# Decay rows moved to ScalarE's DMA queue, with a third raw weight buffer, in a hybrid encoder

## The chip, the core and the metric

The kernel runs on one core of one Trainium2 chip, as one program. The metric is device time in microseconds (us) for one execution, the median of several. Five engines work side by side, each through its own instructions in order: TensorE (PE in the profile; its weight loads are PEld), VectorE (DVE), ScalarE (ACT), GpSimd (POOL) and SyncE (SP), which here only issues DMAs. A DMA may be issued by SP, ACT or POOL, and the instruction that issues it stands in that engine's row like any other.

## The reference, cut to what matters

The program is an encoder of two residual layers over 512 positions of width 1024, in float32. The second ("odd") layer is the one that the change touches. Its input projection gives 24 heads of a bidirectional state-space mixer (SSD) in four groups, and a short gated convolution:

```python
xbc = silu(dw_conv(xbc, conv_w) + conv_b)        # width 5, channels of x, B and C
dA = dt * a;  a_cs = cumsum(dA) in chunks of 128
L = exp(where(tri, a_cs[..., :, None] - a_cs[..., None, :], -inf))
M = (C @ B^T) * L                                # per head and direction
y = M @ X + (states that enter the chunk) ...    # forward + backward + d_skip * x
y = rms_norm(y * silu(z));  out = x + concat(y, short_conv) @ w_out
```

Each entry of L needs the running sum `a_cs` of a head both along rows and along columns. The kernel writes `a_cs` to DRAM once (tile `acs`) and reads each head's two rows (forward and backward, 512 positions each) back into all 128 partitions. That read is the "decay" DMA: `e<-acs`, 512 KB written.

## The kernel before, in words

Weights. Every projection weight is loaded as a slab of 128 x 1024 float32 (`w_raw`, from SP), and split into two parts for TensorE: ACT casts the high part (`w_hi`, line 89). In the odd layer ACT also writes minus the raw slab into `w_lo` (L91) and POOL issues a DMA that adds the raw slab to it (L92). So a raw buffer is free again only when that adding DMA is through. There are two raw buffers (`raw_bufs=2`), three of `w_hi` and of `w_lo`, and every fourth slab of these kinds takes one more pair from the odd layer's pool (`self.more`).

Odd layer. 45 channel tiles go one after the other through `fill`: a projection of 24 matmuls into PSUM (`mm_cm`, L323), and then, for the kinds x, B and C, `conv5`: ACT opens it (L724), DVE adds four taps (L726), ACT takes a tanh (L727), DVE ends it (L728). After the matmuls of the next tile, PE transposes the result (L271 into `sb`). Between the tiles stands the SSD: for each of 24 heads `ssd_factors` makes a 512-wide factor `f`. The decays in `e` get two passes in each of four chunks (ACT L925, DVE L926) and an exponential (ACT L928), `f` starts from `cbm` and `dt` (ACT L920, DVE L921), and DVE multiplies the two (L929). `ssd_pair` then uses the factors of two heads on PE (L942, L958).

Order. A list scheduler sets the order of each engine's instructions when the program is built, from the program's dependencies and its own costs; each engine then runs its list strictly in that order. A wait in front of one instruction holds all that stand behind it on the engine.

Buffers. The decays lie in four `wide` tiles. Before head hh is made, `decays(hh + 2)` issues the loads up to that head from SP's queue. Convolved tiles, their temporaries (`c5`, `c5t`), `sc_h` and some tiles of the end share five buffers of tag `c5`; the factors have four.

Of the kernel before, what the change touches and what calls it, by code (L numbers as in the profile page):

```python
# [6 lines left out]
F32 = mybir.dt.float32  # L7
F32R = mybir.dt.float32r
# [7 lines left out]
P = 128  # L16
S = 512
NT = 4
D = 1024
# [10 lines left out]
SH = 24  # L30
# [36 lines left out]
BY_DMA = ("C", "B", "x", "zc", "h", "gc", "gb", "zd")  # L67
# [3 lines left out]
class Weights:  # L71
# [7 lines left out]
    def _prepare(self):  # L79
        nc = self.tc.nc  # L80
        key, ap, kt, n = self.slabs[self.i]
        eng = nc.vector if key in EARLY or key in ("oe", "oo") and self.i % 2 else nc.gpsimd
        self.i += 1
        raw = self.pool.tile([P, D], F32, name="w_raw", tag="w_raw", bufs=self.raw_bufs)[:, :kt * n]
        nc.sync.dma_start(raw, ap)
        more = key in BY_DMA and self.i % 4 == 0
        hi, lo = ((self.more if more else self.pool).tile([P, D], F32R, name=nm, tag=nm, bufs=1 if more else self.bufs)
                  [:, :kt * n] for nm in ("w_hi", "w_lo"))
        nc.scalar.copy(hi, raw)  # L89
        if key in BY_DMA:  # L90
            nc.scalar.mul(lo, raw, -1.0)  # L91
            nc.gpsimd.dma_start(lo, raw, accum_op=ALU.add)  # L92
        else:
            eng.tensor_tensor(lo, raw, hi.bitcast(F32), op=ALU.subtract)  # L94
        v = lambda t: t.rearrange("p (k n) -> p k n", k=kt)
        self.ready.append((key, v(hi), v(lo)))
# [79 lines left out]
def trunk(ctx, tc, A, out, dbg=None):  # L176
    nc = tc.nc
# [13 lines left out]
    def page(name, tag, dt=F32):  # L191
        return pg.tile([P, S], dt, name=name, tag=tag, bufs=npage[tag])
# [4 lines left out]
    def small(shape, name, bufs=2, dt=F32):  # L197
        return cp.tile(shape, dt, name=name, tag=name, bufs=bufs)
# [26 lines left out]
    def pcs(name, i=None):  # L225
        o, w = PC[name]
        return pc[:, o:o + w] if i is None else pc[:, o + i:o + i + 1]
# [147 lines left out]
    for k in range(KT):  # L375
# [4 lines left out]
        hi, lo = page("xg_hi", "keep", F32R), page("xg_lo", "keep", F32R)  # L380
# [12 lines left out]
    for t in range(NT):  # L393
        for h in range(2):
            j = small([P, S], "junk", bufs=1, dt=BF16)
# [10 lines left out]
    rb = along(r4, "cv")  # L406
# [23 lines left out]
    for nm, o, w in (("q_norm", 0, 384), ("kv_norm", 384, 256)):  # L430
        ss = small([P, 4], "ss")
        rs = small([P, 4], "rs")
        for t in range(NT):
            j = small([P, S], "junk", bufs=1, dt=BF16)
# [6 lines left out]
        for k in range(w // P):  # L441
            tp = transposed([qkv[t][:, o + k * P:o + (k + 1) * P] for t in range(NT)])
            hi, lo = page("cT_hi", "att", F32R), page("cT_lo", "att", F32R)
# [225 lines left out]
    for h in range(2):  # L669
        c = slice(h * S, (h + 1) * S)  # L670
# [37 lines left out]
    def tmp(name, tag, bufs, shape=(P, S), dt=F32):  # L708
        return pg.tile(list(shape), dt, name=name, tag=tag, bufs=bufs)

    def prow(nm):
        return rc[:, RC[nm][0]:RC[nm][0] + RC[nm][1]]
# [6 lines left out]
    def conv5(key, i, c):  # L719

        z = mm_cm(key, xT)
        w = lambda j: pc[:, PC["conv_c_w"][0] + i * 5 + j:PC["conv_c_w"][0] + i * 5 + j + 1]
        d = tmp("c5t", "c5", 5)
        SC.activation(c, z, AF.Identity, scale=w(2), bias=pcs("conv_c_b", i))  # L724
        for j, o, ii in taps5:
            V.scalar_tensor_tensor(c[:, o], z[:, ii], w(j), c[:, o], op0=ALU.mult, op1=ALU.add)  # L726
        SC.activation(d, c, AF.Tanh, scale=0.5)  # L727
        V.scalar_tensor_tensor(c, d, 1.0, c, op0=ALU.add, op1=ALU.mult)  # L728
# [7 lines left out]
    sc = {}  # L736

    def channel_tile(kind, i):
        if kind == "z":
            for t, a in mm_tm("z", xT, 4, GW + NH, four(1)):  # L740
                V.tensor_tensor(dtr[:, t], a[:, GW:GW + NH], prow("dt_bias"), op=ALU.add)
                gate(zg[i][:, t], a[:, :GW])
        elif kind == "zc":
            c = tmp("c5", "c5", 5)
            gate(c, mm_cm("zc", xT))
            turn_later(c, lambda tp: SC.copy(zg[i // 3][:, :, i % 3 * P:(i % 3 + 1) * P], c4(tp)))
        elif kind == "C":
            inp[i]["C"] = tmp("CT", "CT", 2)
            conv5("C", 16 + i, inp[i]["C"])
            inp[i]["x"] = tmp("xs", "xs", 2, (P, NT, GW))  # L750
        elif kind == "B":
            bt = tmp("BT", "BT", 1)
            conv5("B", 12 + i, bt)
            inp[i]["B"] = bt

            def put(tp):
                inp[i]["Bt"] = tmp("Bt", "Bt", 1)
                SC.copy(inp[i]["Bt"], tp)
            turn_later(bt, put)
        elif kind == "x":  # L760
            c = tmp("c5", "c5", 5)
            conv5("x", i, c)
            g, j = divmod(i, 3)
            turn_later(c, lambda tp: SC.copy(inp[g]["x"][:, :, j * P:(j + 1) * P], c4(tp)))
        elif kind == "h":
            sc["h"] = tmp("sc_h", "c5", 5)
            SC.copy(sc["h"], mm_cm("h", xT))
        elif kind == "gc":
            z, hp = mm_cm("gc", xT), sc["h"]
            V.tensor_tensor(hp, z, hp, op=ALU.mult)  # L770
            c = oF[i] = page("oF", "keep")
            SC.activation(c, hp, AF.Copy, scale=cdw[:, i, 1:2])
            for j, o, ii in taps3:
                V.scalar_tensor_tensor(c[:, o], hp[:, ii], cdw[:, i, j:j + 1], c[:, o], op0=ALU.mult, op1=ALU.add)
        elif kind == "gb":
            z = mm_cm("gb", xT)
            V.tensor_tensor(oF[i], z, oF[i], op=ALU.mult)
        else:
            z = mm_cm("zd", xT)
            gate(sc["h"], z)  # L780
            G.tensor_tensor(oF[i], oF[i], sc["h"], op=ALU.mult)
# [18 lines left out]
    d1, d2, d3, dt = (one([P, NT, NH], n) for n in ("d1", "d2", "d3", "dt"))  # L800
# [18 lines left out]
    back = bank("tp")  # L819
    for d in range(2):  # L820
        tp = transposed([d1[:, t, d * SH:(d + 1) * SH] for t in range(NT)], "tp", SH)
        cs = tmp("cs", "c5", 5)[:SH]
        for c in range(NT):
            o, i, z = cs[:, c * P:(c + 1) * P], tp[:, c * P:(c + 1) * P], ident[:SH]
            if d:
                o, i = o[:, ::-1], i[:, ::-1]
            V.tensor_tensor_scan(o, i, z, 0.0, op0=ALU.add, op1=ALU.bypass)
        nc.sync.dma_start(acs[d], cs)
        for c in range(NT):
            T.transpose(back[:, c * NH + d * SH:c * NH + (d + 1) * SH], cs[:, c * P:(c + 1) * P], ident[:SH, :SH])  # L830
# [69 lines left out]
    def decays(n):  # L900

        while len(ahead) <= min(n, SH - 1):
            e = wide("e").rearrange("p (d s) -> p d s", d=2)
            src = acs[:, len(ahead)].rearrange("d (o s) -> o d s", o=1)
            nc.sync.dma_start(e, src.broadcast_to([P, 2, S]))
            ahead.append(e)

    def ssd_factors(g, j, cbm):

        fs = []  # L910
        for i in range(2):
            hh = g * HPG + 2 * j + i
            hf, hb = hh, SH + hh

            decays(hh + 2)
            rb = ahead[hh]
            e, f = rb[:, 0], tmp("f", "f", 4)
            for c in range(NT):
                cc = slice(c * P, (c + 1) * P)
                SC.activation(f[:, cc], cbm[0][:, cc], AF.Copy, scale=dt[:, c, hf:hf + 1])  # L920
                V.scalar_tensor_tensor(f[:, cc], cbm[1][:, cc], dt[:, c, hb:hb + 1], f[:, cc],  # L921
                                       op0=ALU.mult, op1=ALU.add)
            for c in range(NT):
                cc = slice(c * P, (c + 1) * P)
                SC.activation(e[:, cc], rb[:, 0, cc], AF.Identity, bias=nacs[:, c, hf:hf + 1])  # L925
                V.scalar_tensor_tensor(e[:, cc], rb[:, 1, cc], nacs[:, c, hb:hb + 1], e[:, cc],  # L926
                                       op0=ALU.add, op1=ALU.min)
            SC.activation(e, e, AF.Exp)  # L928
            V.tensor_tensor(f, e, f, op=ALU.mult)  # L929
            fs.append(f)  # L930
        return fs

# [50 lines left out]
    def ssd_turn(g):  # L983

        xs = inp[g]["x"]
        for j in range(3):
            i = 3 * g + j
            tp = transposed([xs[:, c, j * P:(j + 1) * P] for c in range(NT)])
            if g < GRP - 1:
                oF[4 + i] = zg[g].rearrange("p c d -> p (c d)")[:, j * S:(j + 1) * S]  # L990
                SC.activation(oF[4 + i], tp, AF.Copy, scale=pcs("ssd_norm", i))
            else:
                hi, lo = tmp("o_hi", *(("c5", 5), ("c5", 5), ("CT", 2))[j], dt=F32R), \
                    tmp("o_lo", *(("c5", 5), ("BT", 1), ("CT", 2))[j], dt=F32R)
                split_psum(hi, lo, tp, pcs("ssd_norm", i))
                last.append((hi, lo))

# [58 lines left out]
    for h in range(2):  # L1056
        c = slice(h * S, (h + 1) * S)
# [98 lines left out]
```

## Time and profile before

| | us |
|---|---|
| median of 3 runs (lowest, highest) | 992.61 (992.29, 994.43) |
| the profiled execution | 995.21 |
| its span in the profile | 993.4 |
| PE, DVE, ACT, POOL busy in the span | 935.8, 694.3, 505.8, 308.4 |

The span is the time from the first to the last instruction in the trace, 1.8 us less than the profiled execution's own time. Matmuls are pipelined in the profile, so a PE that shows as busy need not run at its peak; the granted clock (PEclk, 1.00 is full speed) says how fast it may run. Rows of a timeline give start and duration in us, engine, line, operation, output and inputs, how many instructions were merged, and in brackets how long the engine stood idle just before and what ended that.

### The profile page before, as it was taken

What the parts mean: (1) busy time and instruction counts of PE and PEld (TensorE: products, weight loads), DVE (VectorE), ACT (ScalarE), POOL (GpSimd) and SP (SyncE); (2) the same over time, 40 slices, a digit from 0 to 9 for tenths busy, and PEclk for the clock granted to TensorE, in tenths of its full rate; (3) what the DMA queues carried; (4) which work ended last, traced back from release to release, by engine and by line L of the source; (5) the groups of instructions that cost most, each with busy time, mean ns of one, the idle gap of its engine ahead of it and who ended that gap; (6) DMA issues with size and microseconds to landing.
All of it is one profiled execution on the core that took longest, in us unless ns stands there. A gap on an engine that the chain in (4) does not pass through costs nothing.

```text
span 993.4 us, 12611 instructions
## 1 busy us (share of the span) xinstructions
PE 935.8 (94%) x4528; PEld 754.4 (76%) x4528; DVE 694.3 (70%) x1292; ACT 505.8 (51%) x964; POOL 308.4 (31%) x269
## 2 busy tenths in 40 slices
PE   7899999999999999999997988898999799999996
PEld 7887686686786787888884767777787687888885
DVE  4699989899898998952446678477857658437315
ACT  7646444444454553632334677557657655534312
POOL 0251734626428063551221121121112212125112
PEclk9999999999999999999996989899899989999998
DMA  8213422212203135233367767657756756661222
GB/s 305 102 30 111 57 60 66 62 33 93 70 25 110 62 49 173 64 128 106 118 167 192 174 166 171 148 136 193 180 149 163 189 136 137 170 181 65 105 85 84
DMA packets 48373, 119.57 MB, mean 120 GB/s; under 512 B 12808, under 2 KB 14472, under 8 KB 48312
## 3 DMA queue, kind: packets, MB, share of 16 engines
q1 hardware_dynamic: 41832, 95.19, 30.9%
q0 software_dynamic: 6480, 23.60, 12.7%
q8 instruction: 35, 0.57, 0.2%
q14 instruction: 26, 0.21, 0.1%
HBM read 90.85 MB, written 4.33 MB: 96 GB/s over the span
## 4 chain that ended last, share of the span: by engine, by line
PE 66%; DVE 12%; DMA 11%; ACT 6%; issue 3%; POOL 0%; SPq 0%; DVEq 0%; ACTq 0%; POOLq 0%
PE acc L323 29%; PE acc L350 9%; PE tp L350 5%; PE sb L350 5%; PE sb L534 5%; DMA e<-acs 4%; PE tp L271 4%; DMA w_raw<-in_w_cm_o 3%; PE cv L350 3%; PE acc L571 3%; PE tp L958 2%; ACT w_hi L89 2%; DMA w_lo<-w_raw 1%; DMA w_raw<-in_w_cm_e 1%; PE cv L942 1%
## 5 line engine op out<-in xcount | busy, mean ns | idle before, releaser
L323 PE MATMUL acc<-xT_hi,w_hi 128*128 128x512 f32 x616 | 253.3, 412 | 2.7 <-ACT xT_hi L411 2.7
L323 PE MATMUL acc<-xT_lo,w_hi 128*128 128x512 f32 x616 | 250.0, 407 | 0.2 <-POOL xT_lo L412 0.2
L89 ACT CAST w_hi<-w_raw 128x1024 fp32r<-128x1024 f32 (+7 forms) x139 | 134.6, 969 | 219.7 <-PE acc L323 58.9
L323 PE MATMUL acc<-xT_hi,w_lo 128*128 128x512 f32 x616 | 157.2, 394 | 0.0
L94 DVE TENSOR_TENSOR w_lo<-w_raw,w_hi 128x1024 fp32r<-128x1024 f32 (+6 forms) x74 | 83.2, 1124 | 92.0 <-ACT w_hi L89 83.2
L323 PEld LDWEIGHTS acc<-xT_hi,w_hi 128*128 128x128 f32 x616 | 119.6, 194 | 28.0 <-ACT xT_hi L411 2.9
L323 PEld LDWEIGHTS acc<-xT_lo,w_hi 128*128 128x128 f32 x616 | 119.4, 194 | 25.1 <-POOL xT_lo L412 0.8
L486 DVE SCALAR_TENSOR_TENSOR cv<-u,pc,cv 128x497 f32<-128x497 f32 (+10 forms) x176 | 130.2, 740 | 10.1 <-ACT cv L475 7.7
L323 PEld LDWEIGHTS acc<-xT_hi,w_lo 128*128 128x128 f32 x616 | 116.5, 190 | 24.2
L92 POOL DMA_DIRECT2D w_lo<-w_raw x45 | 39.3, 873 | 226.4 <-ACT w_lo L91 138.5
L94 POOL TENSOR_TENSOR w_lo<-w_raw,w_hi 128x1024 fp32r<-128x1024 f32 (+1 forms) x20 | 48.1, 2406 | 111.7 <-ACT w_hi L89 111.7
L484 POOL TENSOR_TENSOR side<-side 128x510 f32<-128x510 f32 (+3 forms) x56 | 77.8, 1389 | 4.7
L489 POOL TENSOR_TENSOR u<-cs,side 128x512 f32<-128x512 f32 x8 | 11.0, 1372 | 156.3 <-issue 149.1
L538 ACT ACTIVATE p<-sb,mx 128x512 f32<-128x512 f32 x64 | 43.4, 683 | 20.7 <-DVE mx L536 20.4
L483 POOL TENSOR_SCALAR side<-u,pc 128x510 f32<-128x510 f32 (+3 forms) x56 | 51.1, 913 | 4.7
L91 ACT ACTIVATE w_lo<-w_raw 128x1024 fp32r<-128x1024 f32 x45 | 47.6, 1057 | 0.6 <-PE acc L323 0.6
L926 DVE SCALAR_TENSOR_TENSOR e<-e,nacs 128x128 f32<-128x128 f32 x96 | 33.4, 386 | 18.1 <-ACT e L925 18.1
L536 DVE TENSOR_REDUCE mx<-sb 128x1 f32<-128x512 f32 x64 | 41.7, 684 | 3.1 <-PE sb L534 2.5
L726 DVE SCALAR_TENSOR_TENSOR c<-acc,pc,c 128x510 f32<-128x510 f32 (+1 forms) x48 | 35.8, 746 | 11.3 <-ACT c L724 10.7
L925 ACT ACTIVATE e<-e,nacs 128x128 f32<-128x128 f32 x96 | 32.3, 393 | 21.9 <-DMA e<-acs 21.9
L271 PEld LDWEIGHTS tp<-kc,p 128*128 128x128 f32 x256 | 28.9, 140 | 15.4 <-ACT pt L561 10.7
L534 PE MATMUL sb<-k_t,qk_hi 128*128 128x512 f32 (+1 forms) x128 | 39.4, 403 | 0.4 <-DVE k_t L262 0.4
(325 smaller groups left out, 1850.4 us busy)
## 6 DMA issues: line engine op xcount, KB each, us to landing
w_raw<-in_w_cm_o SPq DMA_DIRECT2D x45, 512.0 KB, 3.5
w_lo<-w_raw POOLq DMA_DIRECT2D x45, 512.0 KB, 5.3
w_raw<-in_w_cm_e SPq DMA_DIRECT2D x32, 512.0 KB, 3.5
e<-acs SPq DMA_DIRECT2D x24, 512.0 KB, 5.9
w_raw<-in_w_out_e SPq DMA_DIRECT2D x16, 512.0 KB, 3.5
w_raw<-in_w_out_o SPq DMA_DIRECT2D x16, 512.0 KB, 3.3
xt<-in_xT SPq DMA_DIRECT2D x8, 256.0 KB, 4.2
x_t<-in_x SPq DMA_DIRECT2D x4, 512.0 KB, 5.8
```

Source lines behind the costliest of these rows:

```text
L89: nc.scalar.copy(hi, raw)
L91: nc.scalar.mul(lo, raw, -1.0)
L94: eng.tensor_tensor(lo, raw, hi.bitcast(F32), op=ALU.subtract)
L271: T.transpose(tp[:rows, j * P:(j + 1) * P], b, ident)
L323: T.matmul(a, l, r, start=n == 0, stop=n == 3 * kk - 1)
L350: T.matmul(accs[t][:, :n], l, r, start=k1 == 0 and c == 0, stop=end and c == len(seq) - 1)
L483: G.tensor_scalar(t[:, o], ut[:, i], wt(j), 0.0, op0=ALU.mult, op1=ALU.add)
L484: G.tensor_tensor(side[:, o], side[:, o], t[:, o], op=ALU.add)
L486: V.scalar_tensor_tensor(c[:, o], ut[:, i], wt(j), c[:, o], op0=ALU.mult, op1=ALU.add)
L534: T.matmul(s, l[:, qs], r, start=n == 0, stop=n == 2)
L536: V.tensor_reduce(mx, s, axis=AX.X, op=ALU.max, negate=True)
L538: SC.activation(p, s, AF.Exp, bias=mx, accum_out=sums[:, q:q + 1])
```

## The change

Four things change, all of them in the odd layer:

- the decay rows are loaded by DMAs that ACT issues instead of SP;
- they are loaded three heads ahead: `decays(2)` before the first head, and `decays(hh + 3)` after head hh's multiplication, in place of `decays(hh + 2)` before head hh;
- every third slab of the kinds that the adding DMA serves takes a third raw buffer, from the odd layer's pool;
- `c5` has four buffers instead of five, and `f` three instead of four.

```diff
-        raw = self.pool.tile([P, D], F32, name="w_raw", tag="w_raw", bufs=self.raw_bufs)[:, :kt * n]
+        more = key in BY_DMA and self.i % 3 == 0
+        raw = (self.more if more else self.pool).tile([P, D], F32, name="w_raw", tag="w_raw",
+                                                      bufs=1 if more else self.raw_bufs)[:, :kt * n]
...
-        d = tmp("c5t", "c5", 5)
+        d = tmp("c5t", "c5", 4)
...
-            nc.sync.dma_start(e, src.broadcast_to([P, 2, S]))
+            nc.scalar.dma_start(e, src.broadcast_to([P, 2, S]))
...
-            decays(hh + 2)
+            decays(2)
             rb = ahead[hh]
-            e, f = rb[:, 0], tmp("f", "f", 4)
+            e, f = rb[:, 0], tmp("f", "f", 3)
...
             V.tensor_tensor(f, e, f, op=ALU.mult)
+            decays(hh + 3)
             fs.append(f)
```

The five other places that name `("c5", 5)` change to 4 in the same way. Lines after 84 are two further down in the new file (L905 becomes L907, L925 becomes L927), and those behind the new `decays` call three.

The scheduler makes new lists. Three places show what moves.

The first is SP's list, from the last even-layer stores (`x1d`) to the middle of the odd layer; `acs<-cs` are the two stores that the decay loads read. Before:

```order
L85 DMA w_raw<-in_w_cm_o 128x1024 x5
L828 DMA acs<-cs 24x512
L85 DMA w_raw<-in_w_cm_o 128x1024
L828 DMA acs<-cs 24x512
L85 DMA w_raw<-in_w_cm_o 128x1024
L905 DMA e<-acs 128x2x512 x4
L85 DMA w_raw<-in_w_cm_o 128x1024 x4
L905 DMA e<-acs 128x2x512 x3
```

After:

```order
L87 DMA w_raw<-in_w_cm_o 128x1024 x6
L830 DMA acs<-cs 24x512 x2
L87 DMA w_raw<-in_w_cm_o 128x1024 x34
```

The decay loads are gone from SP, and 34 raw slabs now follow one another there.

The second is ACT's list where the fourth group's C and B tiles are convolved (`CT` and `BT`). Before:

```order
L89 CAST w_hi<-w_raw 128x1024
L724 ACTIVATE CT<-acc,pc 128x512
L91 ACTIVATE w_lo<-w_raw 128x1024
L925 ACTIVATE e<-e,nacs 128x128 x4
L89 CAST w_hi<-w_raw 128x1024
L727 ACTIVATE c5t<-CT 128x512
L928 ACTIVATE e<-e 128x512
L724 ACTIVATE BT<-acc,pc 128x512
```

After:

```order
L907 DMA e<-acs 128x2x512
L726 ACTIVATE CT<-acc,pc 128x512
L93 ACTIVATE w_lo<-w_raw 128x1024
L907 DMA e<-acs 128x2x512
L91 CAST w_hi<-w_raw 128x1024
L729 ACTIVATE c5t<-CT 128x512
L927 ACTIVATE e<-e,nacs 128x128
L726 ACTIVATE BT<-acc,pc 128x512
```

ACT now issues two decay loads here itself, and the first use of the first of them stands five instructions behind its issue, ahead of BT's opening; before, four uses stood ahead of that opening.

The third is ACT's list in the third group, between the openings of two x tiles (`c_6191` and `c_6239` before, `c_6193` and `c_6241` after are the same tiles). Before:

```order
L724 ACTIVATE c_6191<-acc,pc 128x512
L758 COPY Bt<-sb 128x512
L91 ACTIVATE w_lo<-w_raw 128x1024
L89 CAST w_hi<-w_raw 128x1024
L727 ACTIVATE c5t<-c_6191 128x512
L925 ACTIVATE e<-e,nacs 128x128 x2
L724 ACTIVATE c_6239<-acc,pc 128x512
```

After:

```order
L726 ACTIVATE c_6193<-acc,pc 128x512
L93 ACTIVATE w_lo<-w_raw 128x1024
L760 COPY Bt<-sb 128x512
L907 DMA e<-acs 128x2x512
L91 CAST w_hi<-w_raw 128x1024
L729 ACTIVATE c5t<-c_6193 128x512
L927 ACTIVATE e<-e,nacs 128x128
L726 ACTIVATE c_6241<-acc,pc 128x512
```

The decay load is issued between the two openings, and its first use (of the same tile `e`) stands two instructions behind the issue. The fourth group has the same pattern once more, between its second and third x tiles.

More of the change, by code (lines that the diff above doesn't have):

```diff
@@ L743, in channel_tile @@
         elif kind == "zc":
-            c = tmp("c5", "c5", 5)
+            c = tmp("c5", "c5", 4)
             gate(c, mm_cm("zc", xT))
@@ L760, in channel_tile @@
         elif kind == "x":
-            c = tmp("c5", "c5", 5)
+            c = tmp("c5", "c5", 4)
             conv5("x", i, c)
@@ L765, in channel_tile @@
         elif kind == "h":
-            sc["h"] = tmp("sc_h", "c5", 5)
+            sc["h"] = tmp("sc_h", "c5", 4)
             SC.copy(sc["h"], mm_cm("h", xT))
@@ L821, in trunk @@
         tp = transposed([d1[:, t, d * SH:(d + 1) * SH] for t in range(NT)], "tp", SH)
-        cs = tmp("cs", "c5", 5)[:SH]
+        cs = tmp("cs", "c5", 4)[:SH]
         for c in range(NT):
@@ L992, in ssd_turn @@
             else:
-                hi, lo = tmp("o_hi", *(("c5", 5), ("c5", 5), ("CT", 2))[j], dt=F32R), \
-                    tmp("o_lo", *(("c5", 5), ("BT", 1), ("CT", 2))[j], dt=F32R)
+                hi, lo = tmp("o_hi", *(("c5", 4), ("c5", 4), ("CT", 2))[j], dt=F32R), \
+                    tmp("o_lo", *(("c5", 4), ("BT", 1), ("CT", 2))[j], dt=F32R)
                 split_psum(hi, lo, tp, pcs("ssd_norm", i))
```

## The prediction, written before the run

> **What bounds the kernel now.** I read the page first, then PE's stalls, then what held the engines that PE waited for. Of the page, two rows of the chain that ended last (shares of the span, by engine, by line):
>
> ```profile
> PE 66%; DVE 12%; DMA 11%; ACT 6%; issue 3%; POOL 0%; SPq 0%; DVEq 0%; ACTq 0%; POOLq 0%
> PE acc L323 29%; PE acc L350 9%; PE tp L350 5%; PE sb L350 5%; PE sb L534 5%; DMA e<-acs 4%; PE tp L271 4%; DMA w_raw<-in_w_cm_o 3%; PE cv L350 3%; PE acc L571 3%; PE tp L958 2%; ACT w_hi L89 2%; DMA w_lo<-w_raw 1%; DMA w_raw<-in_w_cm_e 1%; PE cv L942 1%
> ```
>
> PE bounds it, but decay rows (4%) and raw slabs (3% in the odd layer) stand in the chain. The question is where PE itself stops for them. In PE's timeline from 560 to 860 us, where the SSD and its tiles run, five stalls stand out, each before the transposes of a convolved tile:
>
> ```profile
> 573.55 1.12 PE L271 MATMUL sb<-kc,c 128*128 128x128 f32 x4 [3.85 <-DVE c L728]
> 602.70 1.08 PE L271 MATMUL sb<-kc,BT 128*128 128x128 f32 x4 [2.61 <-DVE BT L728]
> 628.57 1.11 PE L271 MATMUL sb<-kc,c 128*128 128x128 f32 x4 [3.24 <-DVE c L728]
> 697.15 1.11 PE L271 MATMUL sb<-kc,BT 128*128 128x128 f32 x4 [4.66 <-DVE BT L728]
> 795.56 1.12 PE L271 MATMUL sb<-kc,BT 128*128 128x128 f32 x4 [6.83 <-DVE BT L728]
> ```
>
> Together 21.2 us. DVE is named, but it was late because ACT was. ACT's timeline just ahead of each stall, its waits for a DMA:
>
> ```profile
> 566.24 1.05 ACT L89 CAST w_hi<-w_raw 128x1024 fp32r<-128x1024 f32 x1 [4.03 <-DMA w_raw<-in_w_cm_o]
> 590.63 1.28 ACT L925 ACTIVATE e<-e,nacs 128x128 f32<-128x128 f32 x4 [1.67 <-DMA e<-acs]
> 599.96 1.04 ACT L89 CAST w_hi<-w_raw 128x1024 fp32r<-128x1024 f32 x1 [1.68 <-DMA w_raw<-in_w_cm_o]
> 618.31 0.40 ACT L925 ACTIVATE e<-e,nacs 128x128 f32<-128x128 f32 x1 [1.12 <-DMA e<-acs]
> 624.62 1.04 ACT L89 CAST w_hi<-w_raw 128x1024 fp32r<-128x1024 f32 x1 [1.90 <-DMA w_raw<-in_w_cm_o]
> 626.87 0.40 ACT L925 ACTIVATE e<-e,nacs 128x128 f32<-128x128 f32 x1 [1.20 <-DMA e<-acs]
> 674.08 0.69 ACT L925 ACTIVATE e<-e,nacs 128x128 f32<-128x128 f32 x2 [1.60 <-DMA e<-acs]
> 688.45 1.05 ACT L89 CAST w_hi<-w_raw 128x1024 fp32r<-128x1024 f32 x1 [3.22 <-DMA w_raw<-in_w_cm_o]
> 786.72 1.28 ACT L925 ACTIVATE e<-e,nacs 128x128 f32<-128x128 f32 x4 [6.84 <-DMA e<-acs]
> ```
>
> Stall by stall, ACT's waits and PE's: 4.03 and 3.85; 3.35 and 2.61; 4.22 and 3.24; 4.82 and 4.66; 6.84 and 6.83. The pairs fit: ACT is held by a DMA, the convolution behind it opens late, and PE stands. It has little slack for it: the next tile's matmuls and the four taps of one convolution take
>
> ```profile
> 715.68 5.50 PE acc L323 x24
> L726 DVE SCALAR_TENSOR_TENSOR c<-acc,pc,c 128x510 f32<-128x510 f32 (+1 forms) x48 | 35.8, 746 | 11.3 <-ACT c L724 10.7
> ```
>
> (a row of the chain and one of the groups): 3.0 us of 5.5 go to the taps alone, before ACT's two passes and the last DVE pass. Other ACT waits for DMAs cost PE nothing, such as this one late in the layer, where no convolution follows and PE is busy throughout (ACT's timeline, and busy time by stretch as below):
>
> ```profile
> 882.78 1.05 ACT L89 CAST w_hi<-w_raw 128x1024 fp32r<-128x1024 f32 x1 [8.45 <-DMA w_raw<-in_w_out_o]
> 860.00:900.00 40.00, 40.00 (x205) 33.90 (x204) 22.64 (x38) 16.75 (x29) 14.50 (x11) 1.00 0.59 158
> ```
>
> So I count only the waits that stand ahead of a convolution.
>
> After each stall PE also runs at a lower clock. Busy time in stretches: us, PE, PEld, DVE, ACT, POOL, granted clock, DMA share, GB/s; the last row is an undisturbed stretch:
>
> ```profile
> 568.00:580.00 12.00, 8.15 (x30) 6.19 (x28) 9.16 (x17) 9.80 (x22) 1.72 (x2) 0.72 0.59 132
> 598.00:610.00 12.00, 9.39 (x52) 8.48 (x51) 9.37 (x20) 8.89 (x21) 1.14 (x2) 0.86 0.85 179
> 624.00:640.00 16.00, 12.76 (x62) 11.06 (x62) 8.21 (x18) 9.50 (x16) 2.15 (x2) 0.79 0.66 161
> 690.00:705.00 15.00, 10.34 (x39) 8.19 (x39) 13.99 (x27) 10.55 (x20) 3.00 (x3) 0.77 0.62 147
> 787.00:802.00 15.00, 8.16 (x42) 7.64 (x42) 11.91 (x24) 10.67 (x20) 1.72 (x2) 0.66 0.75 192
> 802.00:830.00 28.00, 27.83 (x147) 23.07 (x145) 18.36 (x39) 15.81 (x31) 5.17 (x5) 1.00 0.51 132
> ```
>
> PE's busy time times the missing clock: 2.3 + 1.3 + 2.7 + 2.4 + 2.8 = 11.4 us at most, since the clock is a mean over the idle part too; 0 at least. I take 8. So 21.2 + 8 = 29 us are there to be won.
>
> The Trainium skill (TensorE: Matmul & The Clock Gate, Part 1: The HAM clock gate) puts the drop to half speed at an idle window of about 3.4 us. This trace differs: idle stretches of 2.61 and 3.24 us also show 0.86 and 0.79. By the Trainium skill's figure only three stalls would cost clock, and the prize would be 21.2 + 5 = 26 us, an estimate.
>
> **The change part by part.** *Third raw buffer.* What SP waited for, 540 to 860 us (total, times, longest), and the prices of the loop (a median from issue to landing; busy and mean ns):
>
> ```profile
> SPq L85 <- DMA w_lo<-w_raw: 239.9, 38, 12.0
> SPq L905 <- DVE f L921: 27.1, 6, 10.1
> SPq L905 <- DVE f L929: 13.6, 5, 3.3
> SPq L905 <- DVE rs_w L250: 4.3, 1, 4.3
> w_raw<-in_w_cm_o SPq DMA_DIRECT2D x45, 512.0 KB, 3.5
> w_lo<-w_raw POOLq DMA_DIRECT2D x45, 512.0 KB, 5.3
> e<-acs SPq DMA_DIRECT2D x24, 512.0 KB, 5.9
> L91 ACT ACTIVATE w_lo<-w_raw 128x1024 fp32r<-128x1024 f32 x45 | 47.6, 1057 | 0.6 <-PE acc L323 0.6
> L92 POOL DMA_DIRECT2D w_lo<-w_raw x45 | 39.3, 873 | 226.4 <-ACT w_lo L91 138.5
> ```
>
> One raw buffer is held for at least 3.5 (load) + 1.05 (cast) + 1.06 (L91) + 0.87 (POOL) + 5.3 (adding DMA) = 11.8 us. Two give one slab per 5.9 us, no faster than PE eats them (5.5), and any delay shows; three give one per 3.9. The raw part of the ACT waits above, 4.03 + 1.68 + 1.90 + 3.22 = 10.8 us, should go. What it triggers is earlier raw loads; ACT's cast then waits for a free `w_hi` instead, when PE has slabs in hand.
>
> *Decays off SP.* The longest stall shows why they were late: SP's timeline there,
>
> ```profile
> 780.01 0.33 SPq L85 DMA_DIRECT2D w_raw<-in_w_cm_o  x1
> 780.44 0.91 SPq L905 DMA_DIRECT2D e<-acs  x2
> ```
>
> the decay load stood behind a raw load that waited for its buffer; ACT wanted it at 779.9 and got it at 786.7. On ACT no raw load is ahead of it. The decay part of the ACT waits, 1.67 + 1.12 + 1.20 + 1.60 + 6.84 = 12.4 us, should mostly go.
>
> *What ACT pays.* Each issue, and the landing (from the line's own answer; min/median/max):
>
> ```profile
> L905 SPq DMA_DIRECT2D e<-acs x24: 359/377/1347, 545.4 to 838.2; - x24
> DMA to landing us min/median/max: 4.7/5.9/10.8
> ```
>
> 24 x 0.377 = 9.0 us on ACT if it issues like SP. Most stand right ahead of an L727 that waits for DVE's taps anyway; on the path between 0 and 9, and I take 2, the nearer to 0.
>
> *New late places.* In ACT's new list most first uses stand behind 6 us or more of ACT's own work. Three stand too close with a convolution's opening behind them, all shown with the change: in the third group a cast and an L727 between (about 1.7 us by 1.05 and the 0.6 of a tanh, perhaps 3 with the taps' wait, against a landing of 5.9, so 3 us late), the same in the fourth group (3), and fourth group's B tile (opening, L91, issue, cast, tanh: about 3.7, so 2.2 late). Together 8.2, with the clock in the proportion 29/21.2 some 11 us; between 0, if the engines wait for other things meanwhile, and 3 x 5.9 = 18. I take 10.
>
> *Fewer c5 and f buffers.* Four c5 hold two tiles with their temporaries, and PE's transposes free the older one before the next tile's matmuls end: nothing, hidden by those 5.5 us. With three `f`, head h waits until PE has used head h - 3; the pair's matmuls come before that in PE's order. The trace has no such wait. If that cover is gone, each of 12 pairs holds ACT once; the nearest row is the 1.90 us of ACT above, so 0 to 23; I take 0, since a whole fill of three tiles lies between two pairs. The memory that these two give up is what the third raw buffer takes.
>
> What is late next is DVE: it is busy 13.99 of the 15.00 us after 690, and the waits of the state matmuls between groups (L889, L895) are not touched.
>
> Sum: -29 + 2 + 10 + 0 = -17 us. Against the profiled execution's own time, 995.21 - 17 = 978; that execution is 2.6 us above the median of 992.61, so for the median I give 976.
>
> **The rivals.** *Everything is won*: the three late places find ACT waiting for DVE anyway, and only the issues stay: -27, 966.
>
> *The waits only move*: the late places cost their upper end of 18 and one pair in four waits for `f` (3 x 1.9 = 6), -29 + 2 + 18 + 6 = -3, or the late places alone take 17, -10; between these 986. For it: first uses two instructions behind an issue. Against: only three of 24.
>
> *The transfers stay as late*: the bytes are the same, and more of them are under way at once. The DMA share is 0.85 in one stretch above. If decays then land like the slowest (10.8), the three places cost 4.9 more each: -17 + 15 = -2 and less clock, 991. Against: 0.51 to 0.66 in others, and 6 us of ACT work ahead of most uses. The Trainium skill speaks for this one (DMA: Bandwidth & Descriptors, Issuing engines are not separate DMA queues): DMAs from different engines share the same 16 engines, and spreading them saves only issue time. No row of this trace shows the two queues side by side.
>
> *Slower*: the waits that SP bore in front of L905, for the multiplication that frees the buffer, now hold ACT: 27.1 + 13.6 + 4.3 = 45 us in the rows above. If all of it falls ahead of convolutions, -29 + 2 + 45 = +18; it decides from 27 us on, and two thirds to all give 995 to 1011, say 1000. For it: a wait on SP held only loads, on ACT it holds everything. Against: SP ran ahead and waited early, ACT reaches L905 after its own work for the following heads.
>
> **How the numbers follow.** About 0.2%, 2 us, can be told from no change. Chances: my sum 0.50 (968 to 984), everything won 0.10, waits only move 0.17, transfers as late 0.08, slower 0.15. Faster 0.77, same 0.08, slower 0.15. The range leaves out the slower case and the best twentieth: 965 to 993.
>
> **What would show it.** Right: PE's five stalls shrink to about three of 2 to 3 us; ACT's waits for `w_raw` from 560 to 860 fall below 3 us in all, those for `e` below 10; the granted clock there rises; DMA issues stand on ACT's queue at 0.4 us. Wrong: L907 on ACT waiting for `f`, L922 for PE's L942, `e` landing in 8 us or more, or new stalls before `BT` and `c`.

## The result, and the profile after

| | before | after |
|---|---|---|
| median of four runs, us (lowest, highest) | 993.52 (992.29, 994.55) | 958.48 (958.10, 959.50) |
| span of the profiled execution, us | 993.4 | 956.7 |
| mean granted TensorE clock | 0.968 | 0.992 |

The ratio is 0.9647, with a 95% interval of 0.9632 to 0.9662: 35.0 us less, where 17 were forecast and the range ended at 965.

The chain of work that ended last, by engine and by line, holds no decay rows any more (they had 4%, and DMA as a whole 11%):

```profile
PE 79%; DVE 13%; DMA 3%; ACT 3%; issue 1%; POOL 0%; SPq 0%; DVEq 0%; ACTq 0%; POOLq 0%
```

What PE waited for between 520 and 860 us (total, times, longest), before:

```profile
PE sb L271 <- DVE BT L728: 14.1, 3, 6.8
PE sb L271 <- DVE c L728: 7.8, 3, 3.9
PE tp L271 <- DVE d L815: 4.3, 1, 4.3
PE tp L889 <- DVE St L895: 3.6, 5, 1.2
```

and after:

```profile
PE tp L273 <- DVE d L817: 4.3, 1, 4.3
PE tp L891 <- DVE St L897: 3.9, 6, 1.2
PE sb L273 <- DVE c L730: 1.6, 3, 1.0
```

The waits for convolved tiles fell from 21.9 us to 1.6. The other two rows stayed. What ACT waited for between 525 and 880 us, before:

```profile
ACT w_hi L89 <- DMA w_raw<-in_w_cm_o: 36.8, 14, 6.2
ACT e L925 <- DMA e<-acs: 21.9, 9, 6.8
ACT w_hi L89 <- PE acc L323: 15.4, 9, 3.7
```

and after:

```profile
ACT w_hi L91 <- PE acc L325: 40.8, 21, 8.7
ACT e L927 <- DMA e<-acs: 5.0, 3, 2.4
ACT w_hi L91 <- DMA w_raw<-in_w_cm_o: 2.6, 2, 2.4
```

ACT waits for PE now, in front of its casts, and hardly for a transfer. The clock is what is left. Here are the stretches between 520 and 860 us in which the granted clock is half (the windows are set at their edges; length, PE busy, clock, DMA share, GB/s), before:

```profile
530.90:551.30 20.40, 17.04 (x45) 0.50 0.79 202
571.80:578.60 6.80, 5.05 (x14) 0.50 0.79 184
602.50:606.00 3.50, 3.31 (x15) 0.51 0.82 178
626.40:633.30 6.90, 4.73 (x18) 0.51 0.78 185
694.70:701.50 6.80, 4.35 (x13) 0.50 0.52 135
790.30:800.50 10.20, 4.94 (x23) 0.50 0.70 180
```

and after, with the whole rest behind it:

```profile
534.50:541.30 6.80, 6.80 (x19) 0.50 0.91 207
541.30:860.00 318.70, 311.17 (x1585) 1.00 0.71 180
```

The first stretch of each lies behind the stall for `d`; the other five of before lie at the five stalls of the prediction. PE's and its weight loads' busy time in the whole span, before and after:

```profile
PE 935.8 (94%) x4528; PEld 754.4 (76%) x4528; DVE 694.3 (70%) x1292; ACT 505.8 (51%) x964; POOL 308.4 (31%) x269
PE 920.2 (96%) x4528; PEld 741.1 (77%) x4528; DVE 696.0 (73%) x1292; ACT 507.7 (53%) x964; POOL 310.1 (32%) x269
```

The 36.7 us between the two spans come out so. Waits for convolved tiles: 21.9 - 1.6 = 20.3. Clock, estimated as half of PE's busy time in the stretches at 0.50: (5.05 + 3.31 + 4.73 + 4.35 + 4.94) / 2 = 11.2 behind the five stalls, and 17.04 / 2 - 6.80 / 2 = 5.1 behind the stall for `d`. Together 36.6. PE's own busy time bears the clock's part out: the same 4528 matmuls took 15.6 us less, against 16.3 by the estimate.

### The profile page after: what moved, and what is told of

It is laid out like the page before. It is cut to its first block, busy times and chain, and to the rows that moved or that the text cites. A ratio compares the mean times of both kernels' runs of the same rounds, so it can differ in the third digit from the quotient of the medians.

```text
span 956.7 us, 12593 instructions
## 1 busy us (share of the span) xinstructions
PE 920.2 (96%) x4528; PEld 741.1 (77%) x4528; DVE 696.0 (73%) x1292; ACT 507.7 (53%) x964; POOL 310.1 (32%) x269
## 3 DMA queue, kind: packets, MB, share of 16 engines
q0 software_dynamic: 6480, 23.60, 13.7%
## 4 chain that ended last, share of the span: by engine, by line
PE 79%; DVE 13%; DMA 3%; ACT 3%; issue 1%; POOL 0%; SPq 0%; DVEq 0%; ACTq 0%; POOLq 0%
PE acc L325 39%; PE acc L352 10%; PE tp L352 5%; PE sb L352 5%; PE sb L536 5%; PE tp L273 5%; PE acc L573 3%; PE cv L352 3%; PE cv L945 2%; PE tp L961 1%; DMA sums_d<-sums 1%; ACT w_hi L91 1%; PE sb L273 1%; DVE w_lo L96 1%; DMA w_raw<-in_w_cm_o 1%
## 5 line engine op out<-in xcount | busy, mean ns | idle before, releaser
L325 PE MATMUL acc<-xT_hi,w_hi 128*128 128x512 f32 x616 | 249.2, 406 | 2.7 <-ACT xT_hi L413 2.7
L325 PE MATMUL acc<-xT_lo,w_hi 128*128 128x512 f32 x616 | 246.7, 401 | 0.1
L325 PE MATMUL acc<-xT_hi,w_lo 128*128 128x512 f32 x616 | 155.1, 391 | 0.0
L325 PEld LDWEIGHTS acc<-xT_hi,w_hi 128*128 128x128 f32 x616 | 116.9, 190 | 27.3 <-ACT xT_hi L413 2.9
L325 PEld LDWEIGHTS acc<-xT_lo,w_hi 128*128 128x128 f32 x616 | 116.8, 190 | 24.5 <-POOL xT_lo L414 0.8
L928 DVE SCALAR_TENSOR_TENSOR e<-e,nacs 128x128 f32<-128x128 f32 x96 | 30.1, 347 | 22.6 <-ACT e L927 22.5
L923 DVE SCALAR_TENSOR_TENSOR f<-cbm,dt,f 128x128 f32<-128x128 f32 x96 | 39.2, 444 | 5.6 <-ACT f L922 5.6
```

The source lines that it names most:

```text
L325: T.matmul(a, l, r, start=n == 0, stop=n == 3 * kk - 1)
```

## The experiments

The first question was which part of the change did it. "Shares" is the prediction's view, in which raw buffer and decays each remove their own waits.

**Fewer buffers alone.**

```diff
-        d = tmp("c5t", "c5", 5)
+        d = tmp("c5t", "c5", 4)
...
-            e, f = rb[:, 0], tmp("f", "f", 4)
+            e, f = rb[:, 0], tmp("f", "f", 3)
```

> The kernel before with four c5 and three f buffers, nothing else. My sum took these at nothing: 993, within 2 us of the kernel before, the same five stalls of PE. The rival, that fewer buffers by themselves change the scheduler's lists and so the time: off by 5 us or more, either way.

993.52 us, ratio 0.9989 (0.9970 to 1.0008). They cost nothing, as summed.

**The third raw buffer added to that**, decays as before.

```diff
+        more = key in BY_DMA and self.i % 3 == 0
+        raw = (self.more if more else self.pool).tile([P, D], F32, name="w_raw", tag="w_raw",
+                                                      bufs=1 if more else self.raw_bufs)[:, :kt * n]
```

> As e1, and the third raw buffer; the decays stay on SP, two heads ahead. Theory 1, each part removes its own share of ACT's waits (raw 10.8, decays 12.4 of 23.2 us) and of the 35 us: about -16, 977; waits for w_raw under 2 us, waits for e still 10 or more. Theory 2, the raw buffer is the root, since the decays were late only because they stood behind a raw load that waited for its buffer: -28 or more, 965 or less, and the waits for e gone too.

976.7 us, ratio 0.9823 (0.9789 to 0.9856): half of the gain. ACT's waits, 525 to 880 us:

```profile
ACT w_hi L91 <- PE acc L325: 43.9, 19, 9.9
ACT e L927 <- DMA e<-acs: 29.4, 15, 6.8
ACT w_hi L91 <- DMA w_raw<-in_w_cm_o: 4.6, 2, 3.6
```

The waits for raw slabs are nearly gone, those for decays are not.

**The decays on ACT's queue, three heads ahead, with two raw buffers** (and the fewer `c5` and `f`).

```diff
-            nc.sync.dma_start(e, src.broadcast_to([P, 2, S]))
+            nc.scalar.dma_start(e, src.broadcast_to([P, 2, S]))
...
-            decays(hh + 2)
+            decays(2)
...
+            decays(hh + 3)
```

> As e1, and the decays on ACT's queue, three heads ahead; two raw buffers as before. Theory 1: about -19, 974; waits for e 5 us or less, waits for w_raw still 10 or more. Theory 2 (the raw buffer is the root): -10 at most, 983 or more. A third theory, that the queue is the root, since SP's raw loads were held in turn by decay loads that waited for DVE (45 us): 965 or less and the waits for w_raw gone too.

995.1 us, ratio 1.0004 (0.9980 to 1.0028): nothing, against the gain that the view of shares had.

```profile
ACT w_hi L89 <- DMA w_raw<-in_w_cm_o: 56.7, 20, 7.2
ACT e L925 <- DMA e<-acs: 5.2, 3, 4.6
```

The waits for `e` went, and those for `w_raw` grew from 40.5 us (fewer buffers alone) to 56.7: the wait only changed its name. So the parts do not add: 17 + 0 became 35.

**The changed kernel with the decays left on SP**, still three heads ahead (`nc.sync.dma_start` again).

> The changed kernel whole, with the decays three heads ahead but issued by SP. If the lookahead and the raw buffer make the gain and the queue is indifferent: 958 to 961. If the queue is what counts: theory 1 gives about 975, with waits for e of 8 us or more on ACT, since SP holds a decay load behind a raw load and a raw load behind a decay load that waits for its buffer.

976.9 us, 0.9832 (0.9813 to 0.9851), the same as with the raw buffer alone. The third head of lookahead is worth nothing on SP. Next, what it is worth on ACT, and what a late load costs there.

**Two ahead at the old place** (`decays(hh + 2)` before head hh, on ACT):

> The changed kernel, but the decay loads keep their old place: decays(hh + 2) ahead of head hh, on ScalarE's queue. Theory A (the queue alone is what counts once a third raw buffer is there; the third head of lookahead is worth nothing): 957 to 962 us, ACT's waits for the decay tile e at most 10 us in all. Theory B (the loads must also be issued a head earlier, since a load on ACT is issued only when ACT gets there): 966 to 972 us, waits for e above 15 us.

956.5 us, 0.9618 (0.9576 to 0.9659): at least as fast as the changed kernel.

**One head later** (`decays(1)`, then `decays(hh + 2)` behind the multiplication), and **two heads later** (`decays(0)`, `decays(hh + 1)`):

> The changed kernel with every decay load one head later: decays(1) first, decays(hh + 2) behind head hh's multiplication, on ScalarE's queue. Theory A (a late landing is hidden, since ACT waits some 41 us for PE in its casts anyway, and a wait for e takes the place of such a wait): 958 to 963 us, though waits for e grow to 10 to 25 us. Theory B (the price in the prediction: about 3 us for each load whose first use stands close behind its issue with a convolution behind it; with a head less of lookahead some six to eight such places instead of three): 972 to 982 us.

> The changed kernel with every decay load two heads later: decays(0) first, decays(hh + 1) behind head hh's multiplication, on ScalarE's queue. Theory A (hidden until the slack is gone): waits for e of 24 loads at 2 to 4 us each, 50 to 90 us, against 41 us of ACT's waits for PE that they can replace: 965 to 985 us. Theory B (each late load costs its wait): 1000 us or more, slower than the kernel before.

957.8 us, 0.9628 (0.9594 to 0.9661), and 964.2 us, 0.9688 (0.9652 to 0.9724). ACT's waits for `e` from 540 to 860 us rose from 5.0 to 11.7 us in the last, and the time by 5.7. Late loads are cheap here.

**Three tiles filled ahead of the dt chain** instead of two (`fill(3)` and `fill(4)` for `fill(2)` and `fill(5)`):

> The changed kernel with three tiles filled ahead of the dt chain instead of two, and four behind it instead of five. Theory A (PE's 4.3 us stall for d and the half-speed clock from 535 to 545 us, about 5 us of lost work, are what is left there, and a third tile covers them): 950 to 955 us, and the granted clock from 530 to 550 us at 0.95 or more. Theory B (the stall only moves: DVE and ACT reach the chain later because of the third tile's own convolution or passes, or the first SSD heads start later and run dry): 957 to 961 us.

957.9 us, 0.9628 (0.9593 to 0.9663). The stall for `d` is still there, 5.3 us, and PE goes on at 533.9 us as in the changed kernel (533.7): in both traces 49 projection matmuls of the layer stand ahead of it, so the third tile wasn't put there.

**The decays on GpSimd's queue** (`nc.gpsimd.dma_start`), the test of "any queue but SP's":

> The changed kernel, but GpSimd's queue issues the decay loads instead of ScalarE's. Theory A (what counts is that a decay load no longer stands in SP's row behind raw loads that wait for a buffer; any other queue will do): 957 to 964 us, though POOL's own row has the adding DMAs, each of which waits for ACT. Theory B (ACT's own queue matters, because ACT itself uses the decays and reaches the issue in step with their use): 970 to 977 us, as with the loads on SP, and waits of ACT for e of 20 us or more.

976.2 us, 0.9834 (0.9806 to 0.9861). Theory A fell: it is no better than SP. ACT's waits from 525 to 880 us, and the loads' own row (ns, first and last start):

```profile
ACT w_hi L91 <- PE acc L325: 44.9, 19, 9.3
ACT e L927 <- DMA e<-acs: 27.5, 13, 4.2
L907 POOL DMA_DIRECT2D e<-acs x24: 724/768/1098, 542.5 to 820.0; - x24
```

**The kernel before with only the queue changed** (two raw buffers, five `c5`, four `f`):

> The kernel before with one word changed: ScalarE issues the decay loads instead of SP (two heads ahead at the old place, two raw buffers, five c5, four f). Theory A (with two raw buffers the raw loop bounds the layer, so the waits for e only turn into waits for w_raw): 988 to 997 us, ACT's waits for e below 10 us and for w_raw above 40 us. Theory B (the null result of the earlier run came from the third head of lookahead or the fewer buffers, not from the raw loop): 974 to 982 us.

998.2 us, 1.0046 (1.0016 to 1.0075): the move alone makes it a little slower.

**The third experiment's kernel, but a raw buffer is let go earlier**: the adding DMA reads `w_hi` in its place.

```diff
-            nc.gpsimd.dma_start(lo, raw, accum_op=ALU.add)
+            nc.gpsimd.dma_start(lo, hi.bitcast(F32), accum_op=ALU.add)
```

> Two raw buffers, decays on ScalarE three heads ahead, fewer c5 and f (the earlier run that gave nothing), and the adding DMA reads w_hi instead of w_raw, so a raw buffer is free after ACT's two passes: 3.5 + 1.05 + 1.06 = 5.6 us per slab and buffer instead of 11.8, with the same DMA bytes. (The low part of these weights is lost by this.) Theory A (how long a raw buffer is held is what kept that run at 995): 957 to 966 us, ACT's waits for w_raw below 10 us. Theory B (the third buffer helps by something else, such as the place of the slabs or the order of the lists, or the bound is the DMA engines themselves): 985 to 996 us.

958.7 us, 0.9648 (0.9609 to 0.9688), with two raw buffers. ACT's waits from 525 to 880 us:

```profile
ACT w_hi L89 <- PE acc L323: 39.5, 20, 8.0
ACT e L925 <- DMA e<-acs: 6.4, 3, 3.2
ACT w_hi L89 <- DMA w_raw<-in_w_cm_o: 1.3, 1, 1.3
```

This kernel leaves out the low part of these weights. The DMA bytes are the same, and its landings are slower (7.2 us median instead of 6.2). So it is how long a raw buffer is held that kept the third experiment at 995. The lists are new here too; that they alone don't do it is shown further down, with two raw buffers and the changed kernel's lists.

**The dt chain's vector operations emitted one tile earlier**, with the loads two ahead:

> The changed kernel with the decay loads two ahead at their old place (the run of 956.5 us) and the dt chain's vector operations emitted behind the first filled tile instead of the second, so that only one of the four taps of C's convolution stands between them on DVE instead of four. Theory A: PE's stall of 4.7 us for d shrinks by two to three taps of 0.74 us with their share of slow clock, 953 to 955 us. Theory B (the chain is held by ACT's cast that waits for a raw slab, and the taps come later instead): 956 to 958 us.

960.8 us, 0.9674 (0.9655 to 0.9694), against 956.5 for the loads two ahead without it: no gain; PE's wait for `d` stayed at 4.9 us.

**Queue or order.** What was left was why ACT's queue helps and GpSimd's does not. The prediction had said that on SP a decay load stands behind raw loads that wait. The longest wait of the kernel before, once more (the waiting pass is shown in the prediction): DVE's multiplication that frees the buffer, and SP's issue, in the timeline:

```profile
778.75 0.68 DVE L929 TENSOR_TENSOR f<-e,f 128x512 f32<-128x512 f32 x1
780.44 0.91 SPq L905 DMA_DIRECT2D e<-acs  x2
```

The buffer is free at 779.43 and the load is issued at 780.44. SP held it for 1.0 us of a wait of 6.84; the rest is the landing. Of the 20 loads that need a used buffer, 15 go out within 0.1 us of the multiplication's end in that kernel, and the others within 2.1. GpSimd's all go out about 0.3 us behind it. Neither queue makes the loads late. On ACT, in the changed kernel, 13 of 20 go out within 0.1 us and the latest 4.3 us after its buffer came free, since ACT stands at another place of its list then: the waits for `e` fell though the loads did not leave sooner. What differs is where the scheduler put the first use. Counting from the starts of issue and first use in the traces, 14 of 24 first uses stand within 8 us of their issue in the kernel before (a landing takes 5.9), 20 with the loads on SP and 19 on GpSimd beside a third raw buffer, but only 7 in the changed kernel. What such a use costs shows in the SP version (976.9 us), where ACT's longest wait for `e` stands ahead of the end of a convolution, and PE's longest for a convolved tile follows:

```profile
688.82 0.40 ACT L927 ACTIVATE e<-e,nacs 128x128 f32<-128x128 f32 x1 [5.80 <-DMA e<-acs]
690.52 1.11 PE L273 MATMUL sb<-kc,c 128*128 128x128 f32 x4 [5.87 <-DVE c L730]
```

The lists changed in every run, so the queue and the order had never been told apart. The next runs hold ACT, DVE and PE to the list of another kernel, by an edge from each instruction to the one that is to follow it:

```diff
+    for names in ORDERS:
...
+        for a, b in zip(names, names[1:]):
+            tc.add_manual_dep(have[b], a, info, reason="pinned")
```

**Loads on SP, the changed kernel's lists**, and the mirror image, **loads on ACT, the lists of the SP version**:

> The decay loads on SP (as in the run of 976.9 us), with three raw buffers, but ACT, DVE and PE are held to the changed kernel's own lists, instruction by instruction. Theory O (the order of the lists is what the move to ACT's queue changed, the queue itself is worth little): 957 to 963 us, ACT's waits for e at most 10 us. Theory Q (the queue itself: on SP a decay load stands behind raw loads that wait for a buffer): 970 to 980 us, waits for e above 20 us.

> The mirror image: the decay loads on ScalarE's queue, three raw buffers, but ACT, DVE and PE are held to the lists of the version with the loads on SP (976.9 us). Theory O: 973 to 980 us, waits for e above 20 us, since first uses still stand right behind the landing. Theory Q: 957 to 965 us.

959.3 us, 0.9632 (0.9588 to 0.9677), and 989.3 us, 0.9934 (0.9909 to 0.9960). ACT's waits for `e` in the two, in that order (525 to 880 us):

```profile
ACT e L927 <- DMA e<-acs: 7.1, 4, 4.6
```

```profile
ACT e L927 <- DMA e<-acs: 25.9, 14, 4.4
```

The waits follow the list, not the queue. With the changed kernel's lists SP's queue is as good as ACT's. The second came out 12 us above the SP version itself (976.9), more than Theory O had. Its trace shows one thing that differs: ACT now waits in front of its issues for the multiplication that frees the buffer. Of the longest such wait, ACT's last work, the multiplication and the issue:

```profile
573.67 1.28 ACT L922 ACTIVATE f<-cbm,dt 128x128 f32<-128x128 f32 x4
578.20 0.68 DVE L931 TENSOR_TENSOR f<-e,f 128x512 f32<-128x512 f32 x1
578.91 0.37 ACTq L907 DMA_DIRECT2D e<-acs  x1
```

ACT is through at 574.95 and issues at 578.91. Counted like this from the trace, six waits make 15.4 us, where the changed kernel has one of 2.1. The 24 issues, 8.8 us at 0.366, now stand on ACT too, as they do in the changed kernel. No run tells how much of the 12 us each of these is worth.

**Two raw buffers with the changed kernel's lists**, loads on ACT and on SP:

> Two raw buffers, decays on ScalarE's queue, fewer c5 and f (the set that gave 995.1 us), but ACT, DVE and PE held to the changed kernel's lists. Theory R (the third raw buffer works by itself, since two give a slab only every 5.9 us): 985 to 1000 us, ACT's waits for w_raw above 40 us. Theory O2 (the third buffer too works mostly through the order of the lists): 958 to 970 us.

> Two raw buffers and the decay loads on SP, as in the kernel before, with fewer c5 and f, but ACT, DVE and PE held to the changed kernel's lists. If the order were everything: 958 to 965 us. If the raw buffer works by itself and the order does the rest: like the run with two raw buffers and the loads on ACT, 985 to 1000 us, or some us more for raw loads that stand behind decay loads on SP.

1001.6 us, 1.0063 (1.0029 to 1.0097), and 993.5 us, 0.9980 (0.9955 to 1.0005). ACT's waits for raw slabs, in the same order:

```profile
ACT w_hi L89 <- DMA w_raw<-in_w_cm_o: 67.1, 20, 7.8
```

```profile
ACT w_hi L89 <- DMA w_raw<-in_w_cm_o: 61.0, 18, 7.8
```

The good lists are worth nothing without the third buffer. Here too the loads on ACT are the slower ones, by 8 us.

**The third raw buffer with the lists of the first run**, which were made for two:

> The third raw buffer alone (fewer c5 and f, decay loads on SP two ahead: the set that gave 976.7 us), with ACT, DVE and PE held to the lists of the version with two raw buffers (993.5 us). Theory R (the buffer works by itself): 974 to 980 us, ACT's waits for w_raw below 10 us. Theory O2 (its gain came with the new lists): 988 to 995 us, though w_raw is there in time, since the waits for e stand where they stood.

971.1 us, 0.9763 (0.9741 to 0.9785).

```profile
ACT e L927 <- DMA e<-acs: 22.6, 14, 3.3
ACT w_hi L91 <- DMA w_raw<-in_w_cm_o: 6.7, 3, 3.6
```

The buffer works by itself, 22 us of it against the 993.5 of the kernel with fewer buffers alone, whose lists these are, and leaves the waits for `e` where the lists have them.

**One place of the changed kernel's lists altered**: ACT's exponential of the dt chain ahead of a cast, and a convolution's taps behind the chain.

> The changed kernel with its own lists, but for one place: ACT's exponential of the dt chain (L804) stands ahead of the cast that waits 3.9 us for a raw slab, and DVE's taps of C's first convolution and one gate product stand behind the chain's last operation (L817). Theory A (PE's stall of 4.3 us for d and the half clock behind it, 5 to 6 us of lost work, are an effect of order): d is ready at about 527 us, before PE asks for it at 529.4, and the time is 948 to 953 us with the granted clock from 530 to 550 us at 0.95 or more. Theory B (the chain's later steps or C's convolution become late instead): 956 to 960 us.

955.7 us, 0.9610 (0.9588 to 0.9632). PE's wait for `d` is gone, and the scan behind it is late instead (520 to 870 us):

```profile
PE tp L832 <- DVE cs L829: 3.2, 1, 3.2
```

The clock gained nothing: in the profiled execution it is half for 13.7 us there, against 6.8 in the changed kernel.

```profile
533.90:547.60 13.70, 13.70 (x36) 0.50 0.54 146
```

It and the run of 956.5 us are the fastest measured; their intervals meet or overlap the changed kernel's.

The runs that bear on the cause, together. "Close" counts first uses within 8 us of their issue; waits are ACT's, 525 to 880 us.

| raw buffers | queue | lists | close | waits for `e`, us | for `w_raw`, us | time, us |
|---|---|---|---|---|---|---|
| 2 | SP | own (before) | 14 | 21.9 | 36.8 | 993.5 |
| 2 | SP | own (fewer buffers alone) | 18 | 26.4 | 40.5 | 993.5 |
| 2 | ACT | own | 2 | 5.2 | 56.7 | 995.1 |
| 2 | ACT | own (only the queue changed) | 1 | 0.8 | 53.5 | 998.2 |
| 2 | SP | of after | 4 | 2.4 | 61.0 | 993.5 |
| 2 | ACT | of after | 4 | 3.9 | 67.1 | 1001.6 |
| 2, let go early | ACT | own | 7 | 6.4 | 1.3 | 958.7 |
| 3 | SP | made for 2 | 19 | 22.6 | 6.7 | 971.1 |
| 3 | SP | own | 20 | 25.7 | 5.2 | 976.9 |
| 3 | GpSimd | own | 19 | 27.5 | 2.3 | 976.2 |
| 3 | ACT | of the SP version | 19 | 25.9 | 4.7 | 989.3 |
| 3 | SP | of after | 7 | 7.1 | 4.9 | 959.3 |
| 3 | ACT | own (after) | 7 | 5.0 | 2.6 | 958.5 |

Two limits stand one behind the other. How long a raw buffer is held comes first: while it binds, a wait for `e` that goes away comes back as one for `w_raw`. Behind it, the first uses that the list puts right behind a landing hold ACT, and with it the convolutions. Only both together bring PE to its own pace.

The first limit is shown by lists held fixed, without the third buffer and with it: 993.5 and 971.1 us with the lists made for two, 993.5 and 959.3 with those of the changed kernel. Of the second it is shown that it lies in the lists. That it is the first uses in them rests on the waits for `e` and on stalls such as the one of 5.87 us; no run moved these uses alone. Their count by itself doesn't set the time: with the loads two heads later 15 are close, but ACT waits only 11.7 us for `e`, and the time is 964.2.

## Why the prediction was wrong, step by step

*PE's stalls, made by ACT's waits for DMAs*: right. 21.9 us of waits for convolved tiles became 1.6.

*The prize, -29*: too small; this is the first term that failed. Stalls were sized rightly (21.2 against 20.3), but the clock was not. Behind the five stalls 11.2 us were lost, nearly the 11.4 that the prediction had as the most, where it took 8; the stall of 2.61 us was followed by half clock like the others. And the half clock behind the stall for `d`, 5.1 us, stood in no term. That makes some 37. Whether these 5.1 us came by the change is open, and some of them may be luck: their length differs between kernels that are equally fast (last section).

*Third raw buffer*: the mechanism was right. The run that lets a raw buffer go early shows that the holding time is the cause, and the buffer alone brought 17 to 22 us, more than its 10.8 us of ACT's waits.

*Decays off SP*: the cause was wrong, though the waits did fall, from 21.9 to 5.0 us. The step that failed is "the decay load stood behind a raw load that waited for its buffer". It was issued 1.0 us after its own buffer came free, and of 20 loads none was held longer than 2.1 us. The move to ACT made the scheduler write another list, and the list made the difference. The Trainium skill (DMA: Bandwidth & Descriptors, Issuing engines are not separate DMA queues) says that spreading transfers over issuing engines saves only issue time. With the lists held the runs agree that ACT's queue gains nothing: 959.3 us on SP and 958.5 on ACT with the changed kernel's lists, 976.9 and 989.3 with those of the SP version, 993.5 and 1001.6 with two raw buffers. The prediction had set this rule down as a rival by another way, in which landings stay late; the median landing is 6.0 us in the first two.

*What ACT pays, +2*: about 0 in the changed kernel (958.5 against 959.3 on SP), although the issues are there. In the other two pairs it is 12 and 8 us, so the term holds for this list alone. The issues and landings of the changed kernel:

```profile
L907 ACTq DMA_DIRECT2D e<-acs x24: 366/366/487, 547.7 to 802.2; - x24
DMA to landing us min/median/max: 4.6/6.0/8.3
```

*New late places, +10*: this is the term that failed most. ACT's timeline at the first of them, in the third group:

```profile
673.58 0.37 ACTq L907 DMA_DIRECT2D e<-acs  x1
675.62 1.06 ACT L91 CAST w_hi<-w_raw 128x1024 fp32r<-128x1024 f32 x1 [1.90 <-PE acc L325]
677.09 0.63 ACT L729 ACTIVATE c5t<-c 128x512 f32<-128x512 f32 x1 [0.40 <-DVE c L728]
680.14 0.41 ACT L927 ACTIVATE e<-e,nacs 128x128 f32<-128x128 f32 x1 [2.42 <-DMA e<-acs]
680.45 0.76 ACT L726 ACTIVATE c<-acc,pc 128x512 f32<-128x512 f32 x1
```

The wait was forecast at 3 us and is 2.42, but PE lost 1.0 us by it at most (the longest wait for a convolved tile above). The prediction counted what stood between issue and use by its duration, and left out that ACT stands there waiting for PE as well, 1.90 us in front of this cast. It also let every late us of ACT reach PE, as in the five stalls of before; here at least 1.4 of the 2.42 us were slack. The fourth group's waits were 0.89 us and none. The two kernels with later loads bear it out: one head later costs nothing, two heads 5.7 us.

*Fewer buffers, 0*: right, 993.5 us.

*The rivals*: "everything is won" was the case, beyond its own number, since its prize was the same -29; at the late places ACT waited for PE first, though, and not for DVE. "Slower" didn't occur: only one wait of ACT, 2.1 us, stands in front of an issue. Its mechanism is real all the same, as the 15.4 us of such waits in the run of 989.3 us show. "The transfers stay as late" is half true in the raw loads, whose median landing rose from 3.5 to 4.8 us; with three buffers nothing waits for it.

So by the spans the sum was -37 with hardly anything given back, where -29 and +12 were written: 8 us of the miss are from the prize, 12 from late places and issues that cost next to nothing.

## What to carry to other kernels

Before a late load is put down to the queue that issues it, look up when its buffer came free: here SP issued it within 0.1 us of that in 15 cases of 20 and within 2.1 in all, and the remedy was the order of the engine that uses it. Where a scheduler writes the lists, a change of queue is a change of lists too, and holding the lists fixed tells the two apart. An engine that issues a load also stands there until the load's buffer is free, so a list made for another queue can cost more than the issues. A single part that measures as nothing may still be half of the gain, when another limit stands in front of it.

## What the runs showed that was not expected

The half clock behind one and the same stall of 4.3 us for `d` lasted differently long: 20.4 us before and 6.8 after (rows above). In the kernel with fewer buffers alone it was 13.7 us behind a stall of 4.4, and 17.1 behind one of 2.5 in the run that lets a raw buffer go early, which is as fast as the changed kernel:

```profile
530.30:544.00 13.70, 9.22 (x26) 0.50 0.79 174
531.90:549.00 17.10, 16.62 (x47) 0.50 0.33 73
```

What ends the slow stretch is not settled: PE was busy throughout from 540 us on in both profiles of the result, and in the one before the change it stayed at half clock until 551.3.

Why the scheduler puts the first uses later when ACT issues the loads is open too; the runs show only that it does, and what it is worth.
